# Token norms and router logits as products with ones, and key transposes in a later place, in a one-layer diffusion block

## The chip, the cores and the metric

One Trainium2 chip, one core. The metric is the device time of one execution in microseconds (us): the median of 3 runs of the kernel before is 1494.91 us (1494.45 to 1495.57). A difference is told in us and in per cent of that.

## The reference, cut to what matters

One layer on 512 latent tokens and 256 context tokens of width 1024, all in float32:

```
h_ctx = modulate(rmsnorm(ctx), shift_c, scale_c);  h = modulate(rmsnorm(x), shift, scale)
parts = h @ w_in                       # q, two forget gates, v, g, u, sv, two merge gates
s_f, s_b = hgrn_final_state(k, logf, v) of the context, one per head and direction
o = hgrn_chunk_scan(q, k, logf, v, s)  # both directions, 4 heads of 128
y = merge(rmsnorm(o)*silu(g) @ w_a, sgu(u, sv) @ w_b) @ w_out
x = x + g_m * y
h2 = modulate(rmsnorm(x), ...);  aff = softmax(h2 @ router_w)      # 16 experts
gate, idx = top_k(aff.T, 64)           # each expert takes its 64 tokens
x = x + g_f * scatter(silu(xs @ w_gate) * (xs @ w_up) @ w_down * gate)
return rmsnorm(x)
```

`rmsnorm` divides a token by the root of the mean of its squares. The context goes only through the forget gates and v, and gives two states of 128x128 per head. The experts' weights are 16 x 3 matrices of 1024x2048: 403 MB of float32, which nothing but these products reads.

## The kernel before, in words

Tokens lie along the free dimension and channels along the 128 partitions, so that x is eight tiles of 128x512. A product of full precision on TensorE is either one float32 matmul, which the trace shows as two instructions, or, for the large projections, three float32r matmuls of a split operand: `mm3` (L193) takes a high and a low part of each side. The high part of a weight is a copy on ScalarE (L183), the low part a subtraction (L184) on the engine that `eng()` (L175) takes in turn from the list `split_eng`. From L757 that list holds GpSimd alone.

The stages, in the order of the program:

1. **Norms and v (L347 to L422).** The squares of x are formed on VectorE, GpSimd and ScalarE, added to two tiles (`Norm`, L228), summed over the partitions by products that have one column of ones (`total`, L252), rooted as a 128x4 tile, and laid out along the free dimension again by `spread` (L264). `keep_warm` (L94) issues products that nobody reads. The first slice of x is scaled by the norm apart (`scaled=True`, L368). Then, slice by slice, `coef_sums`, `coefs`, `mod_high` and `mod_low` form the modulated slice and `v_lats`, `v_ctxs` use it. In this stage VectorE, ScalarE and TensorE keep the written order.
2. **Forget gates and heads (L466 to L764).** `forget(h)` projects the two gates of a head for latents and context. `ev_ctx` (L481) turns a context gate into a key by a scan and a multiplication on VectorE, then transposes it on TensorE (L496) and copies it (L497); L520 multiplies the transposed keys with v to the state of the head. `heads((0, 1))` and `heads((2, 3))` run eight levels of the scan over a pair of heads, mostly on VectorE (L570 to L580), with products on TensorE (L563).
3. **The other projections (L765 to L795).** `group` (L435) is a projection of 512 columns in four pieces, `branch` (L724) one of two pieces. Between them `ada_rest` (L623) sums the rest of the modulation row by row on VectorE, from tiles that a DMA on ScalarE's queue brings, and `ada_sum` (L642) sums a result over the partitions on TensorE.
4. **Output projection and logits (L808 to L835).** Two halves of four 128x512 outputs. `evac_o` (L816) adds an output to x on VectorE (L817), squares it on ScalarE (L819), and multiplies the sum with the router weights (L822) and the square with ones (L823), each into 32 partitions of one PSUM bank `pl`.
5. **Router (L900 to L963).** `lsb` copies `pl`, four transposes turn it to tokens on the partitions (L905), and a softmax, eight rounds of the top eight and a scan give each token its place. They keep the written order.
6. **Experts (L1043 to L1157).** Two experts at a time. Their weights come in tiles of 1 MB through SyncE's queue, in order, into 16 slots and 5 other places; a slot is loaded again when the products that read it are done.

Outside the stretches that keep the written order (the class `InOrder`, L45), the framework's scheduler orders each engine's instructions when the kernel is built: of the instructions that its cost model holds for ready, the one that stands first in the program. The order is then fixed, and an instruction that waits on the chip holds up all behind it on its engine. DMAs of one queue keep the written order.

Of the kernel before, what the change touches and what calls it, by code (L numbers as in the profile page):

```python
# [8 lines left out]
F32 = mybir.dt.float32  # L9
# [3 lines left out]
AF = mybir.ActivationFunctionType  # L13
ALU = mybir.AluOpType
# [3 lines left out]
P = 128  # L18
D = 1024
# [37 lines left out]
def dit_layer(ctx: ExitStack, tc: tile.TileContext, small, rows, xc, ada_mix, ada_w, w_f, w_in, sgu_wt,  # L57
# [241 lines left out]
                        ab[:, 0:2, k:k + 1].broadcast_to([P, 2, 2]), op=ALU.add)  # L299
        V.tensor_scalar(acol[:, k, :], modv[:, k, 1, :], sm[:, O_NM + k:O_NM + k + 1], None, op0=ALU.mult)  # L300

    def mod_high(k, j, scaled=False):
        xv, h, rstd = ((x_lat[k], h_lat[k]), (x_ctx[k], h_ctx[k]))[j] + (rstds[j],)
        sh, sc = modv[:, k, 0, j:j + 1], acol[:, k, j:j + 1]
        if scaled:
            S.activation(h[:, 0], xv, AF.Identity, bias=sh, scale=sc)
            xa = half("xa")
            V.tensor_scalar(xa, xv, sc, None, op0=ALU.mult)
            xv = xa
        else:  # L310
            V.scalar_tensor_tensor(xv, xv, sc, rstd, op0=ALU.mult, op1=ALU.mult)
            S.activation(h[:, 0], xv, AF.Identity, bias=sh)
        return k, j, xv, h

    def mod_low(k, j, xv, h):
# [29 lines left out]
            aws.append(load_aw(k + 1))  # L345

    rstds = [stat[:, 0:T], stat[:, T:TT]]  # L347
    nl = Norm(x_lat, T, 0)
    nl.square(V, 0)
    nl.square(G, 1)  # L350
    nl.square(V, 2)
    nl.square(G, 3)
    nl.add(G, 1, 3)
    nl.square(S, 4, 5, 6, 7)
    nl.add(V, 0, 2, 4, 5, 1, 6)
    nl.begin()
    nl.total(7, False)
    nl.total(0, True)
    keep_warm(4)
    rs = nl.root()  # L360
    split_eng[:] = [V]
    v_part(0)
    ps = spread(rs, T)
    V.tensor_tensor(x_lat[0], x_lat[0], ps, op=ALU.mult)
    cf = {0: coef_copy(coef_sums(0))}
    keep_warm(2)
    coefs(0, *cf[0])
    mod_low(*mod_high(0, 0, scaled=True))  # L368
    nx = Norm(x_ctx, TC, T)
    cf[1] = coef_copy(coef_sums(1))  # L370
    S.activation(rstds[0], ps, AF.Copy)
    nx.square(G, 1, 3)
    split_eng[:] = [G]
    v_part(1)
# [88 lines left out]
    V.tensor_scalar_add(slot_no, ii[:, :CAP], 1.0)  # L463


    qk, tf, s0 = {}, {}, {}  # L466

    t1 = [long_slot(f"t1{i}").rearrange("p (h d t) -> p h d t", h=2, d=2) for i in range(2)]
    s0_all = quarter("s0").rearrange("p (h d c) -> p h d c", h=NH, d=2)
# [1 line left out]
    def forget(h):  # L471
        qk[h] = slot(f"qk{h}")
        tf[h] = t1[h // 2][:, h % 2]
        s0[h] = s0_all[:, h]
        ktc = half("ktc").rearrange("p (d c) -> p d c", d=2)

        def gate(d, dst, ps):
            S.activation(dst, ps, AF.Sigmoid)
            V.tensor_scalar(dst, dst, omlb[:, d, h:h + 1], lb[:, d, h:h + 1], op0=ALU.mult, op1=ALU.add)

        def ev_ctx(d, ps):  # L481
            b = half("fc")
            f, r = b[:, :TC], b[:, TC:]
            kk = half("kc")[:, :TC]
            gate(d, f, ps)
            G.tensor_scalar(kk, f, -1.0, 1.0, op0=ALU.mult, op1=ALU.add)
            if d == 0:
                rev = view(f, TC - 1, [[-1, TC]])
                V.tensor_tensor_scan(view(r, TC - 1, [[-1, TC]]), rev, rev, initial=1.0, op0=ALU.mult, op1=ALU.bypass)
                V.tensor_tensor(kk[:, 0:TC - 1], kk[:, 0:TC - 1], r[:, 1:TC], op=ALU.mult)  # L490
            else:
                V.tensor_tensor_scan(r, f, f, initial=1.0, op0=ALU.mult, op1=ALU.bypass)
                V.tensor_tensor(kk[:, 1:TC], kk[:, 1:TC], r[:, 0:TC - 1], op=ALU.mult)
            pt = bank(ps_m)
            for i in range(2):
                TE.transpose(pt[:, i * P:(i + 1) * P], kk[:, i * P:(i + 1) * P], ident)  # L496
            S.activation(ktc[:, d, :], pt[:, :TC], AF.Copy)  # L497

        banks = [bank(ps_a) for _ in range(2)]
        cb = bank(ps_a)  # L500
        for pc in range(2):
            hl = split(w_f[h, pc * 512:(pc + 1) * 512, :], 4, f"wf{h}_{pc}")
            if pc == 0:
                TE.matmul(cb, zero_r, h_lat[0][:, 0], start=True, stop=False, skip_group_check=True)
            for d in range(2):
                for i in range(4):
                    k = 4 * pc + i
                    wh, wl = (hl[:, z, i, d * P:(d + 1) * P] for z in range(2))
                    mm3(banks[d], wh, wl, h_lat[k][:, 0], h_lat[k][:, 1], k == 0, k == KT - 1)
                    mm3(cb[:, d * TC:(d + 1) * TC], wh, wl, h_ctx[k][:, 0], h_ctx[k][:, 1], False, k == KT - 1, skip=True)  # L510
                if pc == 1:
                    f = tf[h][:, 1 - d, :]
                    gate(d, f, banks[d])
                    G.tensor_scalar(qk[h][:, (2 + d) * T:(3 + d) * T], f, -1.0, 1.0, op0=ALU.mult, op1=ALU.add)
                    ev_ctx(d, cb[:, d * TC:(d + 1) * TC])

        ps = bank(ps_m)
        for d in range(2):
            for c in range(2):
                TE.matmul(ps[:, d * P:(d + 1) * P], ktc[:, d, c * P:(c + 1) * P], v_ctx[c][:, h * P:(h + 1) * P],  # L520
                          start=c == 0, stop=c == 1)
        S.activation(s0[h], ps[:, 0:2 * P].rearrange("p (d c) -> p d c", d=2), AF.Copy)
# [10 lines left out]
    o_sb = slot("o_sb").rearrange("p (t h c) -> p t h c", t=NT, h=NH)  # L533
    o_ss = const.tile([P, NT, NH], F32, tag="o_ss", name="o_ss")

    def heads(hs):
        tb, pyr, pm, ks, toff = {}, {}, {}, {}, {}
        n = T
        for h in hs:
# [8 lines left out]
        for l in range(8):  # L548
# [208 lines left out]
    split_eng[:] = [G]  # L757
    forget(0)
    forget(1)
    group(0, True, query)  # L760
    heads((0, 1))
    forget(2)
    forget(3)
    heads((2, 3))  # L764
    ada_rest(2, 0)  # L765
    u_t = low_slot("u_t").rearrange("p (g t) -> p g t", g=NH)
    svt = low_slot("svt").rearrange("p (t c) -> p t c", t=NT)
    group(2560, True, lambda j, ps: S.activation(u_t[:, j, :], ps, AF.Gelu_apprx_tanh))
    ada_rest(2, 1)
    ada_sum()  # L770
    group(3072, False, sv_evac)
    ada_rest(3, 0)
    ada_sum()
    gate_group(1, 0)
    sgu_mix()
    ada_rest(3, 1)
# [38 lines left out]

    def evac_o(j, ps):  # L816
        V.scalar_tensor_tensor(x1t[j], ps, mod2[:, 0, j:j + 1], x1t[j], op0=ALU.mult, op1=ALU.add)  # L817
        sq = sqs[:, (j % 4) * T:(j % 4 + 1) * T]
        S.activation(sq, x1t[j], AF.Square)  # L819
        if j == 4:  # L820
            tc.keep_in_program_order(S.activation(junk, eps_t, AF.Sqrt))
        TE.matmul(pl[0:32, :], rt_w[:, j, :], x1t[j], start=j == 0, stop=j == KT - 1, tile_position=(0, 0))  # L822
        TE.matmul(pl[32:64, :], ones[:, 0:32], sq, start=j == 0, stop=j == KT - 1, tile_position=(0, 32))  # L823

    for cb_ in range(2):
        banks = [bank(ps_a) for _ in range(4)]
        for pc in range(4):
            hl = split(w_o[pc * 256:(pc + 1) * 256, cb_ * 512:(cb_ + 1) * 512], 2, f"wo{cb_}_{pc}")
            for j in range(4):
# [69 lines left out]

    V, S, TE = (InOrder(tc, e) for e in engines)  # L900
    lsb = mhalf("lsb")
    S.activation(lsb[0:64, :], pl[0:64, :], AF.Copy)
    ps = bank(ps_m)
    for t in range(NT):
        TE.transpose(ps[:, t * 64:(t + 1) * 64], lsb[0:64, t * P:(t + 1) * P], ident[0:64, 0:64])  # L905
    lgp = ps[:, 0:NT * 64].rearrange("p (t e) -> p t e", t=NT)
    S.activation(r2, lgp[:, :, 32], AF.Sqrt, bias=eps_t, scale=1.0 / D)
    S.activation(junk, eps_t, AF.Exp)
# [283 lines left out]
```

## Time and profile before

| | |
|---|---|
| median of 3 runs | 1494.91 us (1494.45 to 1495.57) |
| the profiled execution | 1490.33 us, span 1488.4 us |
| TensorE (PE) busy | 1431.3 us, 96% of the span, 6634 matmuls |
| VectorE (DVE), ScalarE (ACT), GpSimd (POOL) busy | 415.7, 235.4, 219.4 us |
| HBM read | 466.21 MB, 315 GB/s over the span |

Times below are us from the start of the span. A busy matmul row is no full row: a matmul that stands in the pipeline behind another counts as busy. The granted clock of TensorE is given as a share of 2.4 GHz: 1.00 is that, 0.50 is 1.2 GHz. A row of the timeline shows start, length, engine, line, and in square brackets how long the engine had been idle and what released it; L53 stands for all instructions that keep the written order. PEld is the loading of a stationary operand, q behind an engine's name its sequencer.

### The profile page before, as it was taken

What the parts mean: (1) busy time and instruction counts of PE and PEld (TensorE: products, weight loads), DVE (VectorE), ACT (ScalarE), POOL (GpSimd) and SP (SyncE); (2) the same over time, 40 slices, a digit from 0 to 9 for tenths busy, and PEclk for the clock granted to TensorE, in tenths of its full rate; (3) what the DMA queues carried; (4) which work ended last, traced back from release to release, by engine and by line L of the source; (5) the groups of instructions that cost most, each with busy time, mean ns of one, the idle gap of its engine ahead of it and who ended that gap; (6) DMA issues with size and microseconds to landing.
All of it is one profiled execution on the core that took longest, in us unless ns stands there. A gap on an engine that the chain in (4) does not pass through costs nothing. (4 is left out here: it accounts for less than half of the span.)

```text
span 1488.4 us, 16196 instructions
## 1 busy us (share of the span) xinstructions
PE 1431.3 (96%) x6634; PEld 799.2 (54%) x6634; DVE 415.7 (28%) x728; ACT 235.4 (16%) x393; POOL 219.4 (15%) x178
## 2 busy tenths in 40 slices
PE   8998989999899989999999999999999999999997
PEld 6777877787778563343433433443443343443333
DVE  5535868576535150020020020010001011011003
ACT  3422323232232221000000000000000010000003
POOL 2134232433344211010010010010010010000002
PEclk9999999999999999999999999999999999999999
DMA  8312011656454949999999999999999999999997
GB/s 328 100 57 71 15 43 44 191 170 211 142 163 159 405 198 396 419 421 422 421 420 421 421 421 421 421 421 421 421 422 421 421 421 421 421 421 421 421 394 264
DMA packets 99369, 469.37 MB, mean 315 GB/s; under 512 B 8928, under 2 KB 22368, under 8 KB 51168
## 3 DMA queue, kind: packets, MB, share of 16 engines
q1 hardware_dynamic: 88160, 447.77, 75.0%
q10 hardware_dynamic: 11136, 20.57, 4.1%
q8 instruction: 52, 0.85, 0.2%
q14 instruction: 21, 0.17, 0.0%
HBM read 466.21 MB, written 2.10 MB: 315 GB/s over the span
## 5 line engine op out<-in xcount | busy, mean ns | idle before, releaser
L1037 PE MATMUL ps<-w_d,hid 128*64 128x512 f32 x896 | 244.4, 598 | 1.4 <-ACT hid L1030 1.4
L1067 DVE TENSOR_TENSOR hid<-hid,ps 128x512 f32<-128x512 f32 x32 | 21.7, 687 | 467.8 <-PE ps L1018 430.0
L1037 PEld LDWEIGHTS ps<-w_d,hid 128*64 128x64 f32 x896 | 79.3, 136 | 128.6 <-issue 120.7
L1018 PE MATMUL ps<-w_u,xs_odd 128*64 128x512 f32 x512 | 139.9, 598 | 0.0
L978 POOL TENSOR_SCALAR og<-slot_no,pos,aff 128x64 f32<-128x64 f32 x64 | 36.4, 590 | 675.5 <-PE ps L1005 623.4
L1018 PE MATMUL ps<-w_u,xs 128*64 128x512 f32 x480 | 130.2, 597 | 0.1
L1018 PE MATMUL ps<-w_g,xs_odd 128*64 128x512 f32 x512 | 119.7, 597 | 0.0
L1018 PEld LDWEIGHTS ps<-w_u,xs_odd 128*64 128x64 f32 x512 | 53.8, 136 | 82.6 <-issue 77.6
L1018 PE MATMUL ps<-w_g,xs 128*64 128x512 f32 x384 | 90.1, 597 | 0.0
L1018 PEld LDWEIGHTS ps<-w_u,xs 128*64 128x64 f32 x480 | 48.7, 136 | 75.8 <-issue 70.2
L1018 PEld LDWEIGHTS ps<-w_g,xs_odd 128*64 128x64 f32 x512 | 43.9, 137 | 75.3 <-issue 73.5
L1060 ACT ACTIVATE hid<-ps 128x512 f32<-128x512 f32 x32 | 17.3, 598 | 375.2 <-PE ps L1018 362.2
L993 PEld LDWEIGHTS ps<-oh,x 128*128 128x128 f32 x448 | 52.9, 191 | 26.7 <-issue 24.3
L633 DVE SCALAR_TENSOR_TENSOR ac<-ar,s_t,ac 128x512 f32<-128x512 f32 x56 | 55.6, 992 | 32.5 <-DMA ar<-in_ada_w 31.5
L1030 ACT ACTIVATE hid<-ps 128x512 f32<-128x512 f32 x32 | 17.4, 595 | 293.2 <-PE ps L1029 293.2
L1018 PEld LDWEIGHTS ps<-w_g,xs 128*64 128x64 f32 x384 | 33.6, 136 | 56.1 <-issue 54.8
L993 PE MATMUL ps<-oh,x 128*128 128x128 f32 x448 | 59.8, 283 | 1.2 <-ACT hid L1030 1.2
L1096 PE MATMUL ps<-ys,ot 128*128 128x512 f32 x112 | 50.4, 603 | 0.0
L1121 POOL TENSOR_TENSOR acc<-acc,fn 128x512 f32<-128x512 f32 (+1 forms) x8 | 7.8, 1003 | 238.2 <-ACT ys L1119 238.2
L1091 DVE TENSOR_TENSOR ys<-ps,gf_row 128x512 f32<-128x512 f32 x14 | 9.7, 692 | 114.5 <-PE ps L1037 114.5
L1096 PEld LDWEIGHTS ps<-ys,ot 128*128 128x128 f32 x112 | 20.1, 189 | 30.1 <-issue 22.8
L563 PE MATMUL ps<-qk,kp 128*128 128x128 f32 x224 | 32.1, 288 | 4.3 <-ACT kp L556 3.2
(436 smaller groups left out, 2111.5 us busy)
## 6 DMA issues: line engine op xcount, KB each, us to landing
w_g<-in_e_gate SPq DMA_DIRECT2D x127, 1024.0 KB, 19.8
w_u<-in_e_up SPq DMA_DIRECT2D x124, 1024.0 KB, 19.8
w_d<-in_e_down SPq DMA_DIRECT2D x112, 1024.0 KB, 19.8
w<-in_w_in SPq DMA_DIRECT2D x32, 512.0 KB, 3.7
ar<-in_ada_w ACTq DMA_DIRECT2D x64, 256.0 KB, 3.7
wl<-in_e_down SPq DMA_DIRECT2D x28, 512.0 KB, 10.7
aw<-in_ada_mix SPq DMA_DIRECT2D x8, 1024.0 KB, 8.6
wf<-in_w_f SPq DMA_DIRECT2D x8, 512.0 KB, 3.9
```

The source lines that it names most:

```text
L563: TE.matmul(ps[:, sl], lhs, rhs, start=True, stop=True)
L633: V.scalar_tensor_tensor(acc, r, s_k, acc, op0=ALU.mult, op1=ALU.add)
L978: G.tensor_scalar(og[:, s], slot_no, pe, aff[:, t, 2 * p + e:2 * p + e + 1], op0=ALU.is_equal, op1=ALU.mult)
L993: TE.matmul(ps[:, i * P:(i + 1) * P], x1[:, t, k * P:(k + 1) * P], oh[:, t * P:(t + 1) * P], start=t == 0, stop=t == NT - 1)
L1018: TE.matmul(banks[c][es, :], xs[:, k, es], w_got[p, nm, k, e][:, c * 512:(c + 1) * 512], start=k == 0, stop=k == KT - 1, tile_position=(0, ...
L1030: S.activation(hid[:, c], ph, AF.Copy)
L1037: TE.matmul(py[z][es, :], hid[:, c, j * P + e * CAP:j * P + (e + 1) * CAP], w_got[p, "d", 2 * c + j // 2, e][:, j % 2, z * 512:(z + 1) * 512],
L1060: S.activation(hid[:, c], banks[c], AF.Silu)
L1067: V.tensor_tensor(hid[:, c], hid[:, c], banks[c], op=ALU.mult)
L1091: V.tensor_tensor(ys[:, z * 512:(z + 1) * 512], py[z], gf_row[:, z * 512:(z + 1) * 512], op=ALU.mult)
L1096: TE.matmul(ps, ot[:, t * P:(t + 1) * P], ys[:, zs], start=True, stop=True)
L1121: G.tensor_tensor(acc[t][:, a:b], acc[t][:, a:b], fn[:, a:b], op=ALU.mult)
```

## The change

The norm of x is formed by eight products with a 128x128 tile of ones, which put the sum over the partitions on every partition, a root and a reciprocal of 128x512; the first slice goes the way of the others. The transposes of the context keys and the products with v move from `forget` to `ctx_state(h)`, which stands after the next head's `forget`, after the query projection, or, for head 3, after the levels of `heads((2, 3))`. From the third stage the low parts of the weights are formed on GpSimd and VectorE in turn, and two `ada_sum` stand after the projection of column 3072. The logits are formed in two batches of four slices, the odd slices in 64 further partitions of `pl`; `both` is a 128x64 tile with two identities of 64, and a product with it transposes and adds the two halves of `lsb`.

```diff
-    def mod_high(k, j, scaled=False):
...
-        if scaled:
-            S.activation(h[:, 0], xv, AF.Identity, bias=sh, scale=sc)
-            xa = half("xa")
-            V.tensor_scalar(xa, xv, sc, None, op0=ALU.mult)
-            xv = xa
-        else:
...
-    nl = Norm(x_lat, T, 0)
-    nl.square(V, 0)
...
-    nl.add(V, 0, 2, 4, 5, 1, 6)
-    nl.begin()
-    nl.total(7, False)
-    nl.total(0, True)
-    keep_warm(4)
-    rs = nl.root()
     split_eng[:] = [V]
+    ps = bank(ps_m)
+    for k in range(KT):
+        sq = half("nsq")
+        if k % 2 == 0:
+            V.tensor_tensor(sq, x_lat[k], x_lat[k], op=ALU.mult)
+        else:
+            S.activation(sq, x_lat[k], AF.Square)
+        TE.matmul(ps, ones, sq, start=k == 0, stop=k == KT - 1)
+    S.activation(rstds[0], ps, AF.Sqrt, bias=eps_t, scale=1.0 / D)
+    V.reciprocal(rstds[0], rstds[0])
+    cf = {0: coef_copy(coef_sums(0))}
     v_part(0)
-    ps = spread(rs, T)
-    V.tensor_tensor(x_lat[0], x_lat[0], ps, op=ALU.mult)
-    cf = {0: coef_copy(coef_sums(0))}
-    keep_warm(2)
     coefs(0, *cf[0])
-    mod_low(*mod_high(0, 0, scaled=True))
+    mod_low(*mod_high(0, 0))
...
-    S.activation(rstds[0], ps, AF.Copy)
...
-            pt = bank(ps_m)
-            for i in range(2):
-                TE.transpose(pt[:, i * P:(i + 1) * P], kk[:, i * P:(i + 1) * P], ident)
-            S.activation(ktc[:, d, :], pt[:, :TC], AF.Copy)
...
+    def ctx_state(h):
+
+        pt = bank(ps_m)
+        for d in range(2):
+            for i in range(2):
+                TE.transpose(pt[:, (2 * d + i) * P:(2 * d + i + 1) * P], kc[h][:, d, i * P:(i + 1) * P], ident)
+        ktc = half("ktc").rearrange("p (d c) -> p d c", d=2)
+        S.activation(ktc, pt.rearrange("p (d c) -> p d c", d=2), AF.Copy)
         ps = bank(ps_m)
...
-    def heads(hs):
+    def heads(hs, late_ctx=()):
...
+        for h in late_ctx:
+            ctx_state(h)
...
     forget(0)
     forget(1)
+    ctx_state(0)
     group(0, True, query)
+    ctx_state(1)
     heads((0, 1))
     forget(2)
     forget(3)
-    heads((2, 3))
+    ctx_state(2)
+    heads((2, 3), late_ctx=(3,))
+    split_eng[:] = [G, V]
...
     ada_rest(2, 1)
+    group(3072, False, sv_evac)
     ada_sum()
-    group(3072, False, sv_evac)
+    ada_sum()
     ada_rest(3, 0)
-    ada_sum()
...
+    both = masks.rearrange("p l i -> p (l i)").bitcast(F32)[:, 0:64]
+    V.tensor_tensor(both, ident[:, 0:64], ident[:, 64:128], op=ALU.add)
...
-        TE.matmul(pl[0:32, :], rt_w[:, j, :], x1t[j], start=j == 0, stop=j == KT - 1, tile_position=(0, 0))
-        TE.matmul(pl[32:64, :], ones[:, 0:32], sq, start=j == 0, stop=j == KT - 1, tile_position=(0, 32))
+
+    def logits(js):
+
+        for j in js:
+            o = 64 * (j % 2)
+            sq = sqs[:, (j % 4) * T:(j % 4 + 1) * T]
+            TE.matmul(pl[o:o + 32, :], rt_w[:, j, :], x1t[j], start=j < 2, stop=j >= KT - 2, tile_position=(0, o))
+            TE.matmul(pl[o + 32:o + 64, :], ones[:, 0:32], sq, start=j < 2, stop=j >= KT - 2, tile_position=(0, o + 32))
...
+            if cb_ == 1 and pc == 1:
+                logits(range(0, 4))
+    logits(range(4, 8))
...
-    S.activation(lsb[0:64, :], pl[0:64, :], AF.Copy)
+    S.activation(lsb[:, 0:256], pl[:, 0:256], AF.Copy)
+    V.tensor_copy(lsb[:, 256:512], pl[:, 256:512])
...
-        TE.transpose(ps[:, t * 64:(t + 1) * 64], lsb[0:64, t * P:(t + 1) * P], ident[0:64, 0:64])
+        TE.matmul(ps[:, t * 64:(t + 1) * 64], lsb[:, t * P:(t + 1) * P], both, start=True, stop=True)
```

## Rows read from the trace of the kernel before

**Rows 1.** The page, part 2: busy share of the DMA engines in 40 slices.
```profile
DMA  8312011656454949999999999999999999999997
```

**Rows 2.** Windows: stretch, length, busy PE, PEld, DVE, ACT, POOL, clock, DMA share, GB/s.
```profile
212.00:216.00 4.00, 2.70 (x13) 2.73 (x14) 3.94 (x3) 0.38 (x1) 3.36 (x2) 0.67 0.00 0
12.00:13.00 1.00, 0.00 (x0) 0.00 (x0) 0.90 (x2) 0.00 (x0) 0.00 (x0) 0.50 0.98 410
551.00:554.00 3.00, 3.00 (x25) 2.70 (x25) 1.02 (x4) 0.48 (x2) 3.00 (x7) 1.00 0.00 0
```

**Rows 3.** Timeline, SyncE's queue at the first expert.
```profile
558.44 11.10 SPq L168 DMA_DIRECT2D w_u<-in_e_up  x8
```

**Rows 4.** Waits of PE, 0 to 560: total us, times, longest.
```profile
PE ps L496 <- DVE kc L493: 9.0, 3, 3.1
PE ps L496 <- DVE kc L490: 3.9, 3, 2.6
```

**Rows 5.** Timeline, the first 27 us.
```profile
1.45 7.81 PE L96 MATMUL ps<-ident 128*128 128x128 f32 x52 [1.45 <-POOL ident masks.py:199]
...
16.04 0.69 DVE L53 TENSOR_TENSOR wv0h<-wv,wv0h 128x512 fp32r<-128x512 f32 x1 [0.34 <-ACT wv0h L53]
...
22.32 1.29 PE L53 MATMUL ps<-wv0h,hl 128*128 128x512 f32 x3 [0.43 <-ACT hl L53]
22.44 0.59 ACT L53 ACTIVATE stat<-ps 128x512 f32<-128x512 f32 x1
...
24.05 0.16 DVE L53 TENSOR_TENSOR modv<-ps,ab 128x4 f32<-128x4 f32 x1 [0.33 <-PE ps L53]
...
26.60 1.99 PE L53 MATMUL ps<-wv0h,hl 128*128 128x512 f32 x6 [0.46 <-ACT hl L53]
```

**Rows 6.** The page, part 5: a float32 product of 128x512, busy us and mean ns.
```profile
L1096 PE MATMUL ps<-ys,ot 128*128 128x512 f32 x112 | 50.4, 603 | 0.0
```

**Rows 7.** The tile `rs`: ns min/median/max, first and last start, forms.
```profile
L53 DVE RECIPROCAL rs<-rs x2: 165/172/178, 15.5 to 31.1; 128x4 f32<-128x4 f32 x1, 128x2 f32<-128x2 f32 x1
```

**Rows 8.** Timeline, 112 to 116: a key of head 1.
```profile
112.24 2.70 POOL L184 TENSOR_TENSOR w_1h<-w,w_1h 128x1024 fp32r<-128x1024 f32 x1
112.73 2.49 DVE L580 TENSOR_TENSOR pyr<-pyr 128x256 f32<-128x256 f32 x1
...
115.70 0.41 PE L496 MATMUL ps<-ident,kc 128*128 128x128 f32 x2 [2.95 <-DVE kc L493]
```

**Rows 9.** Timeline, 276 to 282: the projection of column 3072.
```profile
276.08 1.05 PE L647 MATMUL ps<-ones,ac 128*128 128x1 f32 x8 [2.81 <-DVE ac L633]
...
281.14 1.06 ACT L183 ACTIVATE w_3h<-w 128x1024 fp32r<-128x1024 f32 x1 [8.07 <-DMA ar<-in_ada_w]
```

**Rows 10.** Waits of DVE, 255 to 480: total us, times, longest.
```profile
DVE ac L633 <- DMA ar<-in_ada_w: 31.5, 19, 3.2
```

**Rows 11.** Timeline: a product in four column groups, then the output projection.
```profile
18.67 1.09 PE L53 MATMUL ps<-aw,s_t 128*32 128x256 f32 x16
...
486.21 0.39 PE L195 MATMUL ps<-mt,wo_3h 128*128 128x512 f32 x1
486.44 0.39 PE L196 MATMUL ps<-mt,wo_3h 128*128 128x512 f32 x1
...
489.08 0.75 DVE L817 SCALAR_TENSOR_TENSOR x1t<-ps,mod,x1t 128x512 f32<-128x512 f32 x1 [14.16 <-DMA x1t<-in_xc]
...
489.88 1.06 PE L822 MATMUL ps<-x1t,rt_w 128*32 128x512 f32 x1 [3.05 <-DVE x1t L817]
...
494.35 0.62 PE L822 MATMUL ps<-x1t,rt_w 128*32 128x512 f32 x1
...
495.67 0.50 PE L197 MATMUL ps<-mt,wo_3h 128*128 128x512 f32 x1
...
527.12 0.50 PE L197 MATMUL ps<-mt,wo_3h 128*128 128x512 f32 x1
```

**Rows 12.** Timeline: the transposes of the logits.
```profile
530.92 0.46 PE L53 MATMUL ps<-ident,lsb 64*128 64x64 f32 x4 [0.68 <-ACT lsb L53]
```

More of the change, by code (lines that the diff above doesn't have):

```diff
@@ L300, in coefs, with mod_high @@
         V.tensor_scalar(acol[:, k, :], modv[:, k, 1, :], sm[:, O_NM + k:O_NM + k + 1], None, op0=ALU.mult)
-    def mod_high(k, j, scaled=False):
+    def mod_high(k, j):
         xv, h, rstd = ((x_lat[k], h_lat[k]), (x_ctx[k], h_ctx[k]))[j] + (rstds[j],)
         sh, sc = modv[:, k, 0, j:j + 1], acol[:, k, j:j + 1]
-        if scaled:
-            S.activation(h[:, 0], xv, AF.Identity, bias=sh, scale=sc)
-            xa = half("xa")
-            V.tensor_scalar(xa, xv, sc, None, op0=ALU.mult)
-            xv = xa
-        else:
-            V.scalar_tensor_tensor(xv, xv, sc, rstd, op0=ALU.mult, op1=ALU.mult)
-            S.activation(h[:, 0], xv, AF.Identity, bias=sh)
+        V.scalar_tensor_tensor(xv, xv, sc, rstd, op0=ALU.mult, op1=ALU.mult)
+        S.activation(h[:, 0], xv, AF.Identity, bias=sh)
         return k, j, xv, h
@@ L347, in dit_layer @@
     rstds = [stat[:, 0:T], stat[:, T:TT]]
-    nl = Norm(x_lat, T, 0)
-    nl.square(V, 0)
[L350 to L354, printed above, removed]
-    nl.add(V, 0, 2, 4, 5, 1, 6)
-    nl.begin()
-    nl.total(7, False)
-    nl.total(0, True)
-    keep_warm(4)
-    rs = nl.root()
-    split_eng[:] = [V]
+    split_eng[:] = [V]
+    ps = bank(ps_m)
[9 more added lines that the diff above has]
+    cf = {0: coef_copy(coef_sums(0))}
     v_part(0)
-    ps = spread(rs, T)
-    V.tensor_tensor(x_lat[0], x_lat[0], ps, op=ALU.mult)
-    cf = {0: coef_copy(coef_sums(0))}
-    keep_warm(2)
     coefs(0, *cf[0])
-    mod_low(*mod_high(0, 0, scaled=True))
+    mod_low(*mod_high(0, 0))
     nx = Norm(x_ctx, TC, T)
     cf[1] = coef_copy(coef_sums(1))
-    S.activation(rstds[0], ps, AF.Copy)
     nx.square(G, 1, 3)
@@ L463, in dit_layer @@
     V.tensor_scalar_add(slot_no, ii[:, :CAP], 1.0)
-    qk, tf, s0 = {}, {}, {}
+    qk, tf, s0, kc = {}, {}, {}, {}
     t1 = [long_slot(f"t1{i}").rearrange("p (h d t) -> p h d t", h=2, d=2) for i in range(2)]
@@ L474, in forget @@
         s0[h] = s0_all[:, h]
-        ktc = half("ktc").rearrange("p (d c) -> p d c", d=2)
+        kc[h] = half("kc").rearrange("p (d t) -> p d t", d=2)
         def gate(d, dst, ps):
@@ L483, in ev_ctx @@
             f, r = b[:, :TC], b[:, TC:]
-            kk = half("kc")[:, :TC]
+            kk = kc[h][:, d, :]
             gate(d, f, ps)
@@ L817, in evac_o @@
         V.scalar_tensor_tensor(x1t[j], ps, mod2[:, 0, j:j + 1], x1t[j], op0=ALU.mult, op1=ALU.add)
-        sq = sqs[:, (j % 4) * T:(j % 4 + 1) * T]
-        S.activation(sq, x1t[j], AF.Square)
+        S.activation(sqs[:, (j % 4) * T:(j % 4 + 1) * T], x1t[j], AF.Square)
         if j == 4:
             tc.keep_in_program_order(S.activation(junk, eps_t, AF.Sqrt))
-        TE.matmul(pl[0:32, :], rt_w[:, j, :], x1t[j], start=j == 0, stop=j == KT - 1, tile_position=(0, 0))
-        TE.matmul(pl[32:64, :], ones[:, 0:32], sq, start=j == 0, stop=j == KT - 1, tile_position=(0, 32))
+    def logits(js):
[4 more added lines that the diff above has]
+            TE.matmul(pl[o + 32:o + 64, :], ones[:, 0:32], sq, start=j < 2, stop=j >= KT - 2, tile_position=(0, o + 32))
     for cb_ in range(2):
```

## The prediction, made before the changed kernel was run

> **What bounds the kernel now.** I read the strip of the DMA engines first: from the 16th slice of 40 to the end they are full [rows 1], so from about 558 us the time is the stream of the experts' weights, and none of the edits touches a byte of it. Next the windows around its beginning: at 551 to 554 the DMA share is 0.00 [rows 2], because all places for weights are filled, and the stream goes on when the first expert's products free one, at 558.44 [rows 3]. What stands before 558.44 is thus a chain through TensorE that ends in that first release, and a microsecond gained or lost there is one at the end. Third, the waits of TensorE in that stretch [rows 4], and the timeline at each.
>
> The sum is made against the profiled execution, 1490.33 us; the median of the runs is 4.58 us more, and the difference is carried over to it.
>
> **Norm of x.** The 52 instructions of the warm-up end at 9.26 [rows 5]. Eight products of 128x512 with ones are 16 instructions of 50.4 / 112 = 0.45 us [rows 6], 7.2 us, so the sum stands at 16.5; the squares are cheap beside that and lie under it. The root of 128x512 costs what a 128x512 copy from PSUM on ScalarE costs, 0.59 [rows 5]: 17.1. The trace has no reciprocal of 128x512. From below it is a pass like the subtraction of 128x512, 0.69 [rows 5]. From above: 128x2 takes 165 ns and 128x4 178 [rows 7], 6.5 ns an element, which for 512 gives 0.165 + 510 x 0.0065 = 3.5 us. I take 3.5, the row of the same operation: 20.6. Behind it VectorE's written order has the subtraction of the first piece of v, 0.69, and then, as for the second slice, 2.55 us from the modulation at 24.05 to the product at 26.60 [rows 5]: the first product stands at 23.8 where it now stands at 22.32, 1.5 us late. With the warm-up products of this stretch gone, TensorE has nothing after two `coef_sums` of 1.09 [rows 11], at 18.7, for 5 us. A stretch without products goes with a clock of 0.50 at 12 to 13 us [rows 2]; the next products run at half clock, of which I put 1.0 us on the path, the rest falling into the wait for the second slice. Sum **+2.5**, bounds -2 (the cheap reciprocal, a warm clock) and +4.
>
> The Trainium skill (VectorE: DVE Perf Modes, First, the fixed hardware budget) says that a reciprocal is an iterated divide with a repeat count of 8. Worked out from that and the clock that the page gives, as an estimate, 512 elements take 512 x 8 / 0.96 GHz = 4.3 us, and this part would be +3.3. The slope of rows 7 stands nearer to that than to a single pass.
>
> **Keys of the context.** Six of the eight transposes wait for VectorE, 9.0 + 3.9 = 12.9 us [rows 4]. One of them shows why: VectorE is held for 2.49 us in a small multiplication that began inside a 2.70 us subtraction on GpSimd, and the key's own multiplication comes behind it, while the transposes stand ahead of other products in TensorE's queue [rows 8]. In the new places each head's keys were ready long before: for heads 0 to 2 a whole `forget` or projection lies between, for head 3 the levels. The number of transposes, products and copies stays (one copy of 512 columns in place of two of 256). After the longest of these waits the clock is 0.67 over 4 us [rows 2]; I add 1 us each for the two waits of the second pair that go with it: 14.9. The 3.1 us wait at 213 stands just before `heads((2, 3))`, where VectorE is busy 3.94 of 4 us [rows 2]; what TensorE gains there is only a lead over a stretch that VectorE sets, so I give that one back: **-12**. Bounds: -15 (all of it) and -6 (only the first pair's, 2 x 2.95 and a short one).
>
> **Splits and sums.** The wait of 2.81 us for `ada_sum` at 276 goes [rows 9]. What is late next is the feed: the copy of the fourth piece of column 3072 starts at 281.14, held on ScalarE behind the DMAs of `ada_rest` [rows 9], and TensorE, 2.8 us earlier, runs up against it. I count **-1**. In the same stretch 22 of 44 low parts go to VectorE, each 2 x 0.69 = 1.4 us, 30 us over some 260 in which VectorE has room; the cover is the lead of a piece over its products. Without that cover each late piece is a wait of TensorE. Bounds -6 (twice the wait at 276) and +8 (a third of a microsecond for each VectorE split).
>
> **Logits.** Now they stand between the products of the output projection. The first waits 3.05 us for x, which a DMA brings late (VectorE idle 14.16) [rows 11], and each slice costs about 1.32 us (494.35 to 495.67) plus what the slow clock adds. Counted from 486.67, 1 + 12 + 96 projection products are left; at the step of 0.23 (486.21 to 486.44) the last would start 108 x 0.23 = 24.8 later, at 511.5. To this comes one batch of 16 instructions: 16 of 256 columns in four column groups took 1.09 [rows 11], so 512 columns 2.1. The late x remains: its first evacuation ends at 489.83, and the first half's products now end at 489.6, which leaves 0.3 of the 3.05. The last product then starts at 513.9 and not at 527.12: **-13.2**. The second batch changes nothing behind it: the last slice's addition, square and product with ones follow one another as before, and the other products of the batch fit into that. If four groups ran no faster than two, the batch would be 4 x 1.32 = 5.3 and the gain 10; from the other side 14. The loads don't eat the gain: their share is 0.00 shortly before the release [rows 2], and the last of them are issued behind the last logits product, so they move with it.
>
> **Transposes of the logits.** Two half copies save about 0.2 of one. Four transposes of 64 rows take 0.46 [rows 12]; four float32 products with a 128-row operand are eight instructions of 7.81 / 52 = 0.15 [rows 5], 1.2 us. **+0.5**, bounds 0 and +1.
>
> The sum is 2.5 - 12 - 1 - 13.2 + 0.5 = -23.2: 1467.1 for the profiled execution, 1471.7 for the median; I predict **1472 us**, with a range of its own of 1462 to 1481.
>
> **Rivals.** (a) The keys' waits don't go, or pass to another: the scheduler puts `ctx_state` as early as before, or VectorE, full in both pairs of heads, ends the same stretch at the same time. For it speaks VectorE's load at 212 [rows 2]; against it that the first pair's waits lie ahead of any heads. The keys then give 4: 1480. (b) TensorE gets ahead of its feed after the heads: pieces come late because ScalarE's queue is held by DMA issues, as at 281 [rows 9]. For it speaks that wait; against it that a low part takes 2.70 us [rows 8] and its 24 products 24 x 0.23 = 5.5 [rows 11]. The splits part is then +8: 1481. (c) Slower than before: VectorE's queue waits 19 times and 31.5 us in all for the rows of `ada_rest` [rows 10], up to 3.2 each, and 22 low parts now stand in that queue. If each came late by 1.6 us, that is 35 us: 1471.7 + 1 + 35 = 1508. It decides from (23.2 + ~1) / 22 = 1.1 us a piece. Against it speaks that a piece is split some microseconds ahead of use. The Trainium skill (SBUF — State Buffer, Who interferes with whom) makes (c) worse: a VectorE instruction with two SBUF inputs and a GpSimd instruction that reads SBUF lock each other out for a whole instruction. By that rule, the trace agrees: the 2.49 us of rows 8. (d) That the logits don't gain: the four groups share one PSUM bank and serialise; at the 5.3 above, 1475, inside my range.
>
> **How the numbers follow.** The forecast with (d) has 0.62, (a) 0.14, (b) 0.12, (c) 0.06; 0.06 is left for sums below 1462, where the wait at 213 or all feed waits also go. 1459 to 1486 holds the forecast, (a), (b) and half of the low tail, a little over 8 in 10 with the sizes unsure. No change is taken to be within 0.2%, 3 us, about what a measurement of this kernel can tell; only a mix of (b) and (c) lands there, 0.03. Slower by more is (c) with what I don't see, 0.07; faster 0.90.
>
> **What would show it.** In the changed kernel: no wait of TensorE at the key transposes; the reciprocal's length and the start of the first v product (23.8); the wait at `ada_sum` gone and the next one, at a weight piece; 13 us less from the first output piece's end to the last logits product, with two groups of 16 instructions of about 2 us; the first release at about 535; from there to the end the same 930 us. A DMA share that does not fall to 0 before that release, or a longer stretch behind it, would overturn the whole sum; a reciprocal under 1 us only its first term.

## The result, and the profile after

The changed kernel takes 1454.88 us (median of 4 runs, 1453.90 to 1456.64) against 1495.24 for the one before in the same comparison: ratio 0.9744, 95% interval 0.9728 to 0.9760. Forecast were 1472 us and a range of 1459 to 1486. The direction was right; the gain is 40 us between the medians and 36.4 between the two profiled executions (1453.95 us, span 1452.0), where 23.2 were forecast, and the time lies below the range.

The end of the program behaves as it did. The strip of the DMA engines, the window in the gap of the stream and SyncE's first issue behind it answer to [rows 1 to 3]:

```profile
DMA  8422012656547979999999999999999999999997
...
518.00:522.00 4.00, 4.00 (x22) 1.65 (x23) 0.41 (x1) 0.24 (x1) 0.00 (x0) 1.00 0.00 0
...
522.25 7.85 SPq L168 DMA_DIRECT2D w_u<-in_e_up  x6
```

The share still falls to 0.00 before the release; that now comes at 522.25 instead of 558.44, and from there to the end of the span it is 929.8 us, before it was 930.0. All of the difference arises ahead of the release. Where, the starts and ends of the same instructions in the two timelines show (us; the lead is after minus before):

| mark | before | after | lead | step | forecast for the step |
|---|---|---|---|---|---|
| last product of v starts | 69.47 | 73.09 | +3.6 | +3.6 | +2.5 |
| last product of the gates ends | 206.60 | 195.03 | -11.6 | | |
| last o of the heads is copied | 261.18 | 247.39 | -13.8 | -17.4 | -12 |
| first product of w_a starts | 443.87 | 420.85 | -23.0 | -9.2 | -1 |
| first product of w_out starts | 467.76 | 444.72 | -23.0 | 0 | |
| last product of w_out ends | 527.63 | 490.61 | -37.0 | -14.0 | -13.2 |
| first expert's product starts | 554.76 | 518.57 | -36.2 | +0.8 | +0.5 |

Two steps are off by more than a microsecond or so: the projections between the heads and w_out, and the heads themselves. The waits of TensorE in that middle stretch, 247 to 455 in the changed kernel (total us, times, longest):

```profile
PE ps L197 <- POOL w_2h L184: 0.7, 1, 0.7
PE ps L197 <- DVE w_1h L184: 0.7, 1, 0.7
PE ps L197 <- DVE w_3h L184: 0.6, 2, 0.4
PE ps L195 <- DVE gt L739: 0.4, 1, 0.4
```

Four kinds of wait, 2.4 us. The wait for `ada_sum` [rows 9] is gone, and so are others that the prediction never named. In the kernel before the same view, 247 to 490 (so that it reaches the first addition of the output projection), reads:

```profile
PE ps L647 <- DVE ac L633: 3.3, 2, 2.8
PE ps L822 <- DVE x1t L817: 3.1, 1, 3.1
PE ps L195 <- DVE gt L746: 2.9, 2, 1.5
PE ps L718 <- DVE o_sb L713: 1.8, 1, 1.8
PE ps L197 <- POOL w_2h L184: 1.8, 2, 1.3
PE ps L196 <- POOL w_1h L184: 0.4, 1, 0.4
PE ps L599 <- ACT kt L595: 0.2, 1, 0.2
```

Of 13.5 us, 11.1 are waits for VectorE, in a stretch in which VectorE is busy for half of the time. So it is not short of time in general; something makes single instructions late. The timeline of the kernel before around one of the waits for `gt` and the one for `o_sb`, and around the load of x (L633 is a row of `ada_rest`, L184 a low part):

```profile
371.15 2.39 POOL L184 TENSOR_TENSOR w_1h<-w,w_1h 128x1024 fp32r<-128x1024 f32 x1 [2.16 <-ACT w_1h L183]
371.33 2.76 DVE L633 SCALAR_TENSOR_TENSOR ac<-ar,s_t,ac 128x512 f32<-128x512 f32 x1
374.01 0.67 DVE L746 TENSOR_TENSOR gt<-gt,ps 128x512 f32<-128x512 f32 x1
374.74 0.50 PE L195 MATMUL ps<-w_0h,hl 128*128 128x512 f32 x1 [1.51 <-DVE gt L746]
...
394.74 4.02 DVE L713 SCALAR_TENSOR_TENSOR o_sb<-o_sb,o_r,gts 128x128 f32<-128x128 f32 x7
395.39 2.43 POOL L184 TENSOR_TENSOR w_1h<-w,w_1h 128x1024 fp32r<-128x1024 f32 x1 [4.49 <-ACT w_1h L183]
...
469.80 2.57 POOL L184 TENSOR_TENSOR wo_1h<-wo,wo_1h 128x1024 fp32r<-128x1024 f32 x1 [4.23 <-ACT wo_1h L183]
470.80 2.12 DVE L755 TENSOR_TENSOR mt<-gt,mt 128x512 fp32r<-128x512 f32 x1
473.56 0.63 ACT L754 ACTIVATE mt<-gt 128x512 fp32r<-128x512 f32 x1 [2.79 <-DVE gt L753]
473.56 1.10 ACTq L171 DMA_DIRECT2D x1t<-in_xc  x2
```

Three times the same picture as in [rows 8]. A row of L633 takes 0.75 us as a rule and 2.76 beside a subtraction on GpSimd; `gt`, behind it on VectorE, is late, and TensorE waits. Seven instructions of L713 take 4.02 us beside one. A 0.69 us subtraction takes 2.12, a copy on ScalarE waits for what stands behind it, and the load of x, behind that copy on ScalarE's queue, leaves late: a part of the 3.05 us wait for x [rows 11]. In the changed kernel the same seven, with no low part on GpSimd beside them:

```profile
373.21 1.92 DVE L706 SCALAR_TENSOR_TENSOR o_sb<-o_sb,o_r,gts 128x128 f32<-128x128 f32 x7
```

Two batches of logits stand where the forecast put them. The first batch in the timeline, its first and last row and the projection product behind it:

```profile
477.55 0.62 PE L828 MATMUL ps<-x1t,rt_w 128*32 128x512 f32 x1
...
478.88 0.59 PE L829 MATMUL ps<-sqs,ones 128*32 128x512 f32 x1
479.40 0.50 PE L195 MATMUL ps<-mt,wo_2h 128*128 128x512 f32 x1
```

That is 1.85 us for 16 instructions, where 2.1 were forecast; four start within 0.02 us and the next four 0.43 later. And the norm, from the sums to the products of v, with the window behind them (length, busy PE, PEld, DVE, ACT, POOL, clock, DMA share, GB/s):

```profile
10.19 7.03 PE L53 MATMUL ps<-nsq,ones 128*128 128x512 f32 x16
17.33 0.69 ACT L53 ACTIVATE stat<-ps,eps_t 128x512 f32<-128x512 f32 x1 [7.34 <-PE ps L53]
18.05 3.35 DVE L53 RECIPROCAL stat<-stat 128x512 f32<-128x512 f32 x1 [8.00 <-ACT stat L53]
23.87 1.58 PE L53 MATMUL ps<-wv0h,hl 128*128 128x512 f32 x3 [3.53 <-ACT hl L53]
...
26.00:32.00 6.00, 6.00 (x16) 4.48 (x16) 4.19 (x10) 1.33 (x3) 0.07 (x1) 0.56 0.82 333
```

The reciprocal and the first product stand where the forecast had them (3.5 us, 23.8). The clock behind them is 0.56 over 6 us; before it was 1.00 over the same six.

### The profile page after: what moved, and what is told of

It is laid out like the page before. It is cut to its first block, busy times and chain, and to the rows that moved or that the text cites. A ratio compares the mean times of both kernels' runs of the same rounds, so it can differ in the third digit from the quotient of the medians.

```text
span 1452.0 us, 16122 instructions
## 1 busy us (share of the span) xinstructions
PE 1417.9 (98%) x6616; PEld 795.0 (55%) x6616; DVE 422.4 (29%) x748; ACT 233.9 (16%) x388; POOL 162.6 (11%) x153
## 5 line engine op out<-in xcount | busy, mean ns | idle before, releaser
L1028 PEld LDWEIGHTS ps<-w_u,xs_odd 128*64 128x64 f32 x512 | 54.7, 136 | 83.6 <-issue 77.9
L1040 ACT ACTIVATE hid<-ps 128x512 f32<-128x512 f32 x32 | 17.4, 596 | 292.8 <-PE ps L1039 292.8
L1028 PEld LDWEIGHTS ps<-w_g,xs 128*64 128x64 f32 x384 | 33.6, 136 | 56.1 <-issue 54.8
L626 DVE SCALAR_TENSOR_TENSOR ac<-ar,s_t,ac 128x512 f32<-128x512 f32 x56 | 48.6, 869 | 24.3 <-DMA ar<-in_ada_w 23.9
L1107 DVE TENSOR_TENSOR acc<-acc,ps 128x512 f32<-128x512 f32 x48 | 33.0, 687 | 9.7 <-PE ps L1106 9.7
L1009 DVE TENSOR_SCALAR xs_odd<-ps,a,mod 128x128 f32<-128x128 f32 x16 | 6.6, 409 | 98.6 <-PE ps L1003 98.6
```

The source lines that it names most:

```text
L626: V.scalar_tensor_tensor(acc, r, s_k, acc, op0=ALU.mult, op1=ALU.add)
L1009: V.tensor_scalar(xs[:, k, :], ps[:, i * P:(i + 1) * P], a2[:, k:k + 1], mod2[:, 1, k:k + 1], op0=ALU.mult, op1=ALU.add)
L1028: TE.matmul(banks[c][es, :], xs[:, k, es], w_got[p, nm, k, e][:, c * 512:(c + 1) * 512], start=k == 0, stop=k == KT - 1, tile_position=(0, ...
L1040: S.activation(hid[:, c], ph, AF.Copy)
L1107: V.tensor_tensor(acc[t][:, zs], x1[:, t, zs] if p == 0 else acc[t][:, zs], ps, op=ALU.add)
```

## The experiments

Two questions stood after this comparison: whether GpSimd's subtractions, by holding up VectorE, are what the splits take away (theory B), or the prediction's feed and its -1 are right and the extra gain lies elsewhere; and whether the keys' gain is partly given back (the prediction) or not (theory A). Each kernel was timed beside the kernel before on the same chip. Single profiled executions of one kernel differ: a second one of the changed kernel has its release at 524.27, 2.0 us later than the first, so differences of rows below 2 us count only where a named wait, or the same difference in several executions, stands behind them.

**One part alone on the kernel before.** Keys first: `ctx_state` with its calls, nothing else.

```diff
     forget(1)
+    ctx_state(0)
     group(0, True, query)
+    ctx_state(1)
     heads((0, 1))
...
-    heads((2, 3))
+    ctx_state(2)
+    heads((2, 3), late_ctx=(3,))
```

> Kernel before, with only the key transposes and state products moved into ctx_state (norm, splits, sums and logits as before). Theory A (from the two traces): nothing is given back. The six waits of 12.9 us go and with them the clock that they cost, 3.1 us over 132 to 261 (clock 0.98 x 75 and 0.97 x 54): -16 to -17 against before. Rival (the prediction): the wait at 213 comes back because the second pair of heads is set by VectorE: -12. Second rival: the extra beyond 12 in the changed kernel came from elsewhere (the longer norm had left a lead): -8 or less. No wait over 0.3 us at the transposes in any of them.

Measured 1477.65 against 1493.16 us, ratio 0.9896 (0.9880 to 0.9912): -15.5 us. By the rows the release came 14.4 earlier, of which 1.1 is an earlier start of v that has nothing to do with the keys: -13.3. Theory A's size fits, its mechanism doesn't. In place of the wait at 213 the second pair of heads has new ones:

```profile
195.75 3.50 PE L567 MATMUL ps<-q_t,ks 128*128 128x128 f32 x16 [2.21 <-POOL ks L548]
...
204.29 1.20 PE L567 MATMUL ps<-qk,kp 128*128 128x128 f32 x8 [1.46 <-DVE qk L574]
```

From the last product of the gates to the last copied o it takes 54.8 us here and took 54.6 before, though a wait of 3.06 is gone from it. That is the give-back that the prediction counted.

**Only the second pair of keys**, to see that give-back apart from the first pair.

```diff
     forget(0)
+    ctx_state(0)
     forget(1)
+    ctx_state(1)
     group(0, True, query)
...
-    heads((2, 3))
+    ctx_state(2)
+    heads((2, 3), late_ctx=(3,))
```

> Kernel before, with ctx_state used for all heads, but for heads 0 and 1 placed straight behind their own forget, as before; only the second pair is moved. Theory A: the first pair keeps its two waits of about 3 us (the transposes of both directions now stand together, so perhaps only the later one remains), the second pair's 6.4 us and the clock of its two waits go: about -8 to -10. Rival (the prediction): the second pair gives 6.4 + 2 - 3.1 = -5.3, because VectorE sets its end.

Measured 1486.30, ratio 0.9959 (0.9945 to 0.9972): -6.9, between the two; the interval, -4.2 to -8.2, holds the prediction's 5.3 and of theory A only the edge. The stretch of the second pair is 54.8 us again, with 1.45 for `ks` and 1.29 for `qk` in it. Theory A is dropped: the wait at 213 only changed its name.

**Only the splits.**

```diff
     heads((2, 3))
+    split_eng[:] = [G, V]
```

> Kernel before, with only split_eng = [G, V] from behind heads((2, 3)): every second low part on VectorE. Theory B: GpSimd's 2.4 us subtractions hold VectorE's two-input instructions (7 of L713 in 4.02 us with one beside it, in 1.92 without), and that made gt, o_sb and w_2h late; with half of them gone the waits of 1.35, 1.51, 1.83, 1.28 and 0.51 us go in the main: -4 to -6. Rival (the prediction): the feed takes it, 0 to -1. Second rival: VectorE's queue gets late behind the ada_rest rows: slower.

Measured 1480.03, ratio 0.9916 (0.9901 to 0.9932): -13.1, more than any theory had. Waits of TensorE, 247 to 490:

```profile
PE ps L647 <- DVE ac L633: 1.4, 1, 1.4
PE ps L195 <- DVE gt L746: 1.4, 2, 1.1
PE ps L197 <- DVE w_1h L184: 0.7, 1, 0.7
...
PE ps L197 <- POOL w_2h L184: 0.4, 1, 0.4
```

The wait for `o_sb` is gone, and that for x, which theory B had left out: x is issued 3.9 us behind the first product of w_out instead of 5.8, since the copy ahead of it waits 1.36 and not 2.79 for VectorE. All waits of this view are 5.5 us where they were 13.5. These 8.0, a wait of 1.39 for `kp` in the heads that goes too, and the clock of the output projection (1.00 where it was 0.97 over 60 us: 1.8) make 11.2, and by 11.1 the stretch from v to the release is shorter; the 13.1 of the medians (10.2 to 14.8) are 2 us more, which no row shows. Of the waits, those with VectorE's rows behind them (`ac`, x, `gt`, `o_sb`) fall from 11.1 to 2.8, those for GpSimd's own low parts from 2.2 to 0.4, and VectorE's new low parts bring 1.4.

**Only the sums.**

```diff
+    group(3072, False, sv_evac)
     ada_sum()
-    group(3072, False, sv_evac)
+    ada_sum()
     ada_rest(3, 0)
-    ada_sum()
```

> Kernel before, with only the two ada_sum moved behind the projection of column 3072. Theory C: the wait of 2.81 us and the slow clock after it (0.94 over 27 us, 1.6 us) go, and nothing is late in their place: -4 to -5. Rival (the prediction): the fourth piece of column 3072 is copied late behind the DMAs of ada_rest, and takes 2 to 3 of it: -1 or less. A third: it goes only together with the split on VectorE: 0 here.

Measured 1492.60, ratio 0.9998 (0.9985 to 1.0011): nothing. The wait at 276 is gone, and the sum waits in its new place. Two things make it late there: the last three rows of the sum start 3.11 us after VectorE fell idle, since their tile lands late, and then take 4.32 us, where three rows take 2.25 as a rule, beside GpSimd's squares (L660). The window behind shows the clock:

```profile
288.37 4.32 DVE L633 SCALAR_TENSOR_TENSOR ac<-ar,s_t,ac 128x512 f32<-128x512 f32 x3 [3.11 <-DMA ar<-in_ada_w]
289.20 5.39 POOL L660 TENSOR_TENSOR sq<-svt 128x512 f32<-128x512 f32 x4
292.74 0.49 PE L647 MATMUL ps<-ones,ac 128*128 128x1 f32 x3 [3.24 <-DVE ac L633]
...
292.00:297.00 5.00, 4.26 (x15) 3.68 (x16) 4.92 (x9) 1.06 (x1) 4.92 (x4) 0.63 0.55 185
```

The prediction's reason was another one: it is not the fourth weight piece that is late, but the sum itself. The third view, that the place pays only together with the splits, is taken up below.

**Only the logits** (the two batches, the two half copies, the tile `both`; as in the diff of the change).

> Kernel before, with only the logits in two batches of four column groups (and the copy, the sum tile and the products that transpose them). Prediction: -13.2 + 0.5 = -12.7, 0.3 us of the wait for x left. Theory B, by which the wait of 3.05 us for x belongs to the splits on GpSimd (the load of x stands on ScalarE's queue behind a copy that waits 2.79 us for VectorE): the wait can still appear here, now at the addition before the batch, where nothing is behind it: -12 to -14 as well, and together with the splits the two parts overlap by about 3 us.

Measured 1479.94 against 1493.48, ratio 0.9913 (0.9893 to 0.9933): -13.5, with no wait over 0.3 us in the output projection. This term held.

**One part undone in the changed kernel.** The old norm:

```diff
-    ps = bank(ps_m)
-    for k in range(KT):
...
-    V.reciprocal(rstds[0], rstds[0])
+    nl = Norm(x_lat, T, 0)
...
+    rs = nl.root()
```

> Changed kernel, but with the norm of before (squares added, one column of ones, 128x4 root, spread, first slice scaled apart). Theory D: the new norm costs 3.6 us by the end of v (v ends 73.1 where it ended 69.5), and this lead is kept to the end: 3 to 4 us faster than the changed kernel, -40 to -44 against before. Rival: the later stages take it back, since the loads of v's blocks or of the gates set the pace: same as the changed kernel.

Measured 1451.52, ratio 0.9724 (0.9700 to 0.9748). The changed kernel has 0.9744 and, run again on this chip, 1455.86 us and 0.9745 (0.9722 to 0.9768): 3 to 4 us faster by the medians, though the intervals overlap. The first product of v waits 0.44 us and not 3.53, v's last product starts 3.1 and 2.1 us ahead of the two executions of the changed kernel, and the release comes before either:

```profile
22.83 1.28 PE L53 MATMUL ps<-wv0h,hl 128*128 128x512 f32 x3 [0.44 <-ACT hl L53]
...
518.02 1.65 SPq L168 DMA_DIRECT2D w_u<-in_e_up  x2
```

It is the fastest version here by the medians; the new norm is the one large part of the change that costs.

**The new norm with its gap filled.**

```diff
     cf = {0: coef_copy(coef_sums(0))}
+    keep_warm(16)
     v_part(0)
```

> Changed kernel with 16 more warm-up products (64 instructions, nobody reads them) between the sums of the first modulation and the first product of v, in the gap of 5 us in which TensorE waits for root, reciprocal and modulation. Theory D2: of the 3.6 us of the new norm 1.5 is the later first product and 2.1 the half clock behind the gap; with TensorE at work the clock stays up and about 2 us of the 3.6 come back, v then ends at about 71. Rival: the half clock hides under the wait for the second slice, and nothing changes in v's end (within 0.5 us).

Measured 1453.12, ratio 0.9738 (0.9713 to 0.9762). The same window as above, now at full clock:

```profile
26.00:32.00 6.00, 5.34 (x39) 3.28 (x37) 3.85 (x10) 2.24 (x5) 0.00 (x0) 1.00 0.68 251
```

The first product starts at 23.52, hardly earlier, and v's last product 2.2 us earlier than in the first execution of the changed kernel. So of 3.6 us about 2 are the half clock, and the rest the later first product. The times agree (-1.8), but are too close to carry it alone. The other profiled executions do: from its first to its last product v takes 47.2 us in all seven with the norm of before and 47.4 here, but 48.6 to 49.2 in the six with the new norm and an open gap. The half clock thus costs 1.4 to 2.1 us.

**No low part on GpSimd at all.**

```diff
-    split_eng[:] = [G, V]
+    split_eng[:] = [V]
```

> Changed kernel with split_eng = [V] from the third stage: no low part on GpSimd there. Theory B (the harm is GpSimd's subtraction locking VectorE): the remaining waits with GpSimd's name (0.75 us at w_2h) and those at VectorE's stretched rows go, VectorE gets 22 x (1.22 us) more but is at most 72% busy: 0 to -2 against the changed kernel. Rival (it is a matter of two engines sharing the load): VectorE alone gets late behind the ada_rest rows, +2 to +8.

Measured 1463.46, ratio 0.9803 (0.9779 to 0.9827): 8 us slower than the changed kernel. What stretches VectorE's rows is nevertheless shown by it. The tile `ac` on VectorE, ns min/median/max of its 56 rows, in the kernel before, in the changed kernel and here:

```profile
L633 DVE SCALAR_TENSOR_TENSOR ac<-ar,s_t,ac x56: 739/752/2762, 264.2 to 438.2; 128x512 f32<-128x512 f32 x56
...
L626 DVE SCALAR_TENSOR_TENSOR ac<-ar,s_t,ac x56: 736/751/2300, 250.5 to 413.3; 128x512 f32<-128x512 f32 x56
```

```profile
L626 DVE SCALAR_TENSOR_TENSOR ac<-ar,s_t,ac x56: 739/751/754, 247.4 to 420.5; 128x512 f32<-128x512 f32 x56
```

Without subtractions on GpSimd not one of 56 rows is longer than 754 ns. In the kernel before, 13 of the 56 take over 0.8 us. Each of these lies beside a subtraction on GpSimd and ends 0.55 us after that one's end: the row gets on when GpSimd is done.

What makes the kernel slower is the rival, as far as the rows show it: the pieces now stand in one queue with the rows of `ada_rest`. TensorE waits 6.0 us between the heads and w_a (2.4 for `gt`, 2.2 for weight pieces), where it waits 3.2 in the second execution of the changed kernel. The slow clock takes 6.8 us from the heads of the second pair to w_a and 3.4 there. The windows on either side of the first late piece:

```profile
260.86 0.79 PE L196 MATMUL ps<-w_1h,hl 128*128 128x512 f32 x1 [1.31 <-DVE w_1h L184]
...
256.00:260.80 4.80, 3.45 (x19) 2.61 (x17) 3.17 (x6) 1.72 (x2) 0.00 (x0) 0.97 0.70 219
260.80:265.00 4.20, 4.14 (x12) 3.31 (x13) 3.34 (x6) 0.40 (x1) 0.00 (x0) 0.62 0.86 236
```

**The changed kernel again, and three further parts undone beside it.**

> The changed kernel once more, beside the three that undo one part of it: the yardstick of this group. 0.974 of before, as measured.

1455.86 against 1492.91, ratio 0.9745 (0.9722 to 0.9768). First undone, the splits (the added line of the third experiment taken out):

> Changed kernel with every low part of the third stage on GpSimd again. Theory B: the splits alone gave -13.1 on the kernel before, of which about 3 is the wait for x, which the batches of logits take away too; so 9 to 11 slower than the changed kernel, the mean row of the ada_rest sums at about 0.99 us, and waits of TensorE at ada_sum (as in the kernel with the sums alone moved), gt and o_sb. Rival (the prediction, splits about nothing): within 1 of it.

Measured 1467.09, ratio 0.9829 (0.9804 to 0.9854): 11.2 slower, about what theory B had; the mean row of the sums is 952 ns (0.99 was expected). The waits of the kernel before are back, and the first of them shows the whole chain in three rows:

```profile
258.43 2.36 POOL L184 TENSOR_TENSOR w_1h<-w,w_1h 128x1024 fp32r<-128x1024 f32 x1 [9.27 <-ACT w_1h L183]
258.99 2.35 DVE L626 SCALAR_TENSOR_TENSOR ac<-ar,s_t,ac 128x512 f32<-128x512 f32 x1 [0.50 <-DMA ar<-in_ada_w]
261.40 0.83 PE L640 MATMUL ps<-ones,ac 128*128 128x1 f32 x6 [1.78 <-DVE ac L626]
```

Then the places of the sums (the edit of the fourth experiment, backwards):

> Changed kernel with the two ada_sum in their old places. Theory C2: a place alone moved the wait and gave nothing on the kernel before; with the splits halved the rows come earlier, and in the old place a wait of 1.4 us was left (the kernel with the splits alone), which cost its clock too: 1.5 to 3 slower than the changed kernel. Rival: the place gives nothing here either, 0.

Measured 1458.46, ratio 0.9763 (0.9740 to 0.9786): 2.6 slower, with a wait of 1.43 us at the sum. So the place seems to be worth something only once the splits are halved; the intervals of the two kernels overlap, and it is the wait alone that speaks for this.

Last, the batches of logits in two column groups:

```diff
-            o = 64 * (j % 2)
+            o = 0
...
-    S.activation(lsb[:, 0:256], pl[:, 0:256], AF.Copy)
-    V.tensor_copy(lsb[:, 256:512], pl[:, 256:512])
+    S.activation(lsb[0:64, :], pl[0:64, :], AF.Copy)
...
```

> Changed kernel with the two batches of logits, but in two column groups and 64 partitions as before (copy and transposes of the logits as before). If the gain of 13 us comes from four groups: a batch takes twice its 1.9 us, so +1.9 for the first batch, +2 for what of the second stands behind the last addition: +2 to +4. If it comes from the place (no product waiting between the projection's products): only the first 1.9 is lost, and the transposes give up to 1 back: +1 to +2. If the groups don't run side by side at all: 0.

Measured 1455.82: no difference in the time. The rows show the first batch at almost double length:

```profile
478.23 0.62 PE L828 MATMUL ps<-x1t,rt_w 128*32 128x512 f32 x1
...
481.26 0.59 PE L829 MATMUL ps<-sqs,ones 128*32 128x512 f32 x1
481.78 0.50 PE L195 MATMUL ps<-mt,wo_2h 128*128 128x512 f32 x1
```

3.55 us and not 1.85, with two instructions per 0.43 and not four. From the first product of w_out to the one-hot products the stretch is 71.4 us against 69.9 in the changed kernel beside it (69.2 in its first execution), 1.5 to 2.3 more, which these medians can't tell from none (an interval is 7 us wide). So the gain of 13 us comes from the place of the batches; the four groups are worth about 2 us of it at the most.

## Why the prediction was wrong

**Bound: right.** The stream of weights sets the end from the first release on, and a microsecond ahead of it is one at the end: 36.2 at the release, 36.4 in the span.

**Splits and sums, -1: this is the step that failed.** Alone the splits gave -13.1; undone they cost 11.2; the place of the sums gave 0 alone and 2.6 beside the splits. The prediction asked what 22 new low parts cost VectorE (1.4 us each by its estimate, 1.22 measured) and what covers them. It put at nothing, without a reason, what the 22 that leave GpSimd had cost VectorE: up to 2.0 us in each row that they fall beside. The picture was in [rows 8], and the prediction used it twice: for the keys, and in rival (c), where the lock is held against the change. The rule quoted there (the Trainium skill, SBUF — State Buffer, Who interferes with whom) says that a VectorE instruction with two SBUF inputs contends with a GpSimd instruction that reads SBUF. The traces agree: 2762 ns for the longest row before, 754 without GpSimd. By these rows a subtraction that leaves GpSimd takes a stretched row of VectorE away, and the forecast counted it with the sign turned round.

That the splits give 11 to 13 us is shown from both sides. That all of it is this lock is argued: 1.8 us are GpSimd's own late pieces, which half the load brings in time, late tiles of `ada_rest` have a part in the waits for the sum, and no run takes the lock away while it leaves each engine its load.

With that the next claim fell too, that the feed takes back what the sum gives (the copy at 281 of [rows 9]): at the fourth piece of column 3072 TensorE doesn't wait in the kernel with the splits alone, and 0.4 us at the most in the two executions of the changed one. What the sum's place alone meets is a tile that lands late and the next locked rows.

**Keys, -12: right in its mechanism, a little small.** -13.3 by the rows, -15.5 (13.1 to 17.9) by the medians. No transpose waits any more. The 3.1 us at 213 were given back, as forecast. In the changed kernel the table above shows 17.4 for this stretch; the second pair of heads is 52.4 us long there and 54.7 in the same kernel without the splits, so some 2 us of it belong to the splits again, whose first pieces fall into the heads (53.3 in the second execution of the changed kernel, so 1.4 to 2.3). A further part is work that moved: 12 instructions of heads 2 and 3, transposes and products with v that start 0.11 us apart, stood before the end of the gates and now stand behind it, where TensorE waits for VectorE anyway. That is 1.3 us; the rest of the 17.4 is not traced to a row.

**Logits, -13.2, and their transposes, +0.5: right.** -14.0 in the trace and -13.5 alone. The cause was named in part only: of the 3.05 us for x a share belongs to GpSimd's subtraction ahead of the load, so that splits and logits overlap there. Rival (d), that the groups serialise, is refuted by the 1.85 us.

**Norm, +2.5: right in sign, kind and size; its parts were off.** Against the one profiled execution of the kernel before it is 3.6, but the last product of v starts at 72.2 us in the mean of six executions with the new norm (71.1 to 73.1) and at 69.6 in seven with the old (68.4 to 70.2): 2.6. The half clock was priced at 1.0 and cost 1.4 to 2.1; the later first product was priced at 1.5 and cost 0.8 in the mean. The reciprocal takes 3.35 us (forecast 3.5). The estimate of 4.3 worked out from the Trainium skill's repeat count (VectorE: DVE Perf Modes, First, the fixed hardware budget) is 28% too long. That the first product stands at 23.87 where 23.8 was forecast is partly luck: the sums start at 10.19 and not at 9.26, and from the end of the reciprocal, 21.40, it is 2.5 us and not 3.2.

**The rivals.** (a) did not happen for the first pair and was already in the sum for the second. (b) and (c) did not happen with two engines; in the kernel with VectorE alone pieces do come late in VectorE's queue, as (c) feared, and it is 8 us slower, so that the risk was real. The range ended at 1459 because only 0.06 was left for sums below 1462, and these were thought of as the wait at 213 or feed waits that vanish. The chance of more gain was set by what had a name; the list of all TensorE waits of the stretch, 13.5 us with 11.1 on VectorE, would have given it one.

The parts add up: 3.6 - 15.5 - 13.1 - 0 - 13.5 = -38.5 (the norm by the two timelines, the others by the medians of each alone), where the whole gives -40.4 and, in the second comparison, -37.1. Each of these has an interval of some us, so that an overlap of two parts by 2 or 3 us would not show in this sum.

## What to carry to other kernels

When work moves from one engine to another, price both ends: what the instruction costs where it goes, and what it did to its neighbours where it was. A stretched row (a 0.75 us operation that takes 2.7) beside a GpSimd subtraction is a cost of GpSimd, wherever it is booked. Before forecasting a stage, list all waits of the bounding engine in it, with the engine that they name, and not only those that the change speaks of; and where one engine is to take all of the work, expect its queue to bind: half and half beat either whole here.

## What the runs showed of the hardware that was not expected

- A short wait of TensorE can cost more than its length: behind one of 1.31 us the clock was 0.62 over 4.2 us, behind one of 3.24 it was 0.63 over 5, and both stretches were busy with products. At 0.62 those 4.2 us do the work of 2.6, which is 1.6 us more on a wait of 1.31. It need not: in the kernel before, the clock stayed at 1.00 over the 5 us behind a wait of 2.95 (the first transposes at 92.25) and behind that of 1.51 at 374.74, so a wait has to be priced by the window behind it.

```profile
92.30:97.30 5.00, 5.00 (x31) 4.42 (x32) 1.89 (x7) 0.77 (x2) 0.00 (x0) 1.00 0.37 105
374.80:379.80 5.00, 5.00 (x22) 4.15 (x23) 0.62 (x2) 1.06 (x1) 2.17 (x1) 1.00 0.31 98
```

- float32 products of 32x512 outputs run side by side in four column groups though all write one PSUM bank: four instructions every 0.43 us, and with two groups two every 0.43.
- Filling a gap of TensorE with products that nobody reads kept the clock behind it at 1.00 where it had been 0.56 over 6 us (0.56 to 0.80 in the six executions without them).
